# A hybrid decoder block on one core: another order in the opening, whole residual rows and spaced row work at the block ends

## The chip, the core and the metric

The kernel runs on one core of one Trainium2 chip. The metric is device time in microseconds (us) of one execution. The core has a matrix engine (PE, with its weight loads PEld), a vector engine (DVE), a scalar engine (ACT), a general engine (POOL), and a sync engine (SP) whose queue issues nearly all DMAs here. Each engine takes its instructions in the order of its own queue and a waiting instruction holds those behind it.

## The reference, cut to what matters

Two thousand and forty-eight tokens of width 1024 pass one decoder block: a gated mixer of two branches, then a feed-forward part, each with a norm before and after and with scales, shifts and gates made from one conditioning vector `c`.

```python
mod = c @ w_ada + b_ada
shift_m, scale_m, gate_m, shift_f, scale_f, gate_f = split(mod, 6)
h = modulate(rms_norm(x, g_pre_mix), shift_m, scale_m)
q_a, k_a, v_a, q_m, k_m, v_m, o_m, i_m, f_m, g_a, g_m = split(h @ w_in)
q_a, k_a = rope(q_a, positions), rope(k_a, positions)
y_a = sliding_window_attention(q_a, k_a, v_a, attn_sinks)
q_m, k_m = split(silu(causal_depthwise_conv(concat(q_m, k_m), conv_w, conv_b)))
y_m = sigmoid(o_m) * head_layer_norm(mlstm_chunkwise(q_m, k_m, v_m, i_m, f_m), mlstm_norm_w)
mix = (sigmoid(g_a) * (y_a @ w_branch_attn) + sigmoid(g_m) * (y_m @ w_branch_mlstm)) @ w_out
x = x + gate_m * rms_norm(mix, g_post_mix)
h2 = modulate(rms_norm(x, g_pre_ffn), shift_f, scale_f)
x = x + gate_f * rms_norm((silu(h2 @ w_ffn_gate) * (h2 @ w_ffn_up)) @ w_ffn_down, g_post_ffn)
```

## The kernel before, in words

**Tiling.** The mixer runs over four blocks of 512 tokens (`block(b)`); each is four tiles of 128 tokens. The feed-forward part follows over two blocks of 1024 tokens. Every large product is made in three matmuls: weights and activations are split into a rounded part (`whi`, `hhi`) and the rest (`wlo`, `hlo`), and `mm3` adds hi·hi, hi·lo and lo·hi. ACT casts the rounded part (L233, L236), DVE subtracts for the rest (L234, L237), and PE needs both. PSUM holds four `acc` banks and four `mix` banks. SBUF pools used here: nine `big` buffers of 1 MB, six `tx` buffers of 256 KB, nine `tm`, two `raw` weight buffers, four split buffers.

**Order.** A list scheduler sets the order of each engine's queue from the program's order; instructions wrapped in `pin` keep their place. All matmuls and the first rows of block 0 are pinned; later work is interleaved by `spawn`/`tick`: a generator is resumed when the planner's clock `now` (which `mm` and `transpose` advance) has passed the time that it last yielded.

**The opening.** `FirstRows` prepares block 0. Its inputs are `x_first` (two loads of 1 MB), the first eight halves of the conditioning matrix `ada_first` (tile i = 0..3, two halves of 1 MB each: rows k = 0..3 and 4..7 of eight), and `w_q_vm` in pieces of 1 MB. For each tile i the scale and shift of two feature columns (2i, 2i+1) are needed. Part of the eight rows is multiplied on PE as one-column matmuls (`on_pe`, L460: "columns", 128x1 in the profile), part on DVE as an accumulation over 512 elements (`on_v`, L474: L479 for the first term, L482 for the others). `biased` (L468) adds the bias to the PE part, `sums` (L484) adds the DVE accumulation over partitions by four one-column matmuls against `ones` and finishes s1 and sh1 on DVE (L490 to L492), `turned` (L494) transposes the normalised x of the two feature columns on PE, `rows` (L500) applies scale and shift on ACT (L503 gives `hhi`, L506 the unrounded value), `rest` (L508) makes `hlo` on DVE (L510), `cast` and `weights` (L512, L516) split the weights (L514 on ACT, L519 on DVE). `warm(n)` issues n matmuls of `ones` against `ones`. `begin` runs all this for tile 0; `first_group` (L312) then runs the weight matmuls of four pieces (two feature columns each) in thirds hi·hi, lo·hi, hi·lo of eight, and calls `beside(si, third, j)` after every four, which prepares tile si + 1 between them. Each float32 matmul (columns, `ones`, transposes aside) stands in the trace as two records.

**The block end.** `stage5` ends the mLSTM branch, `stage6` starts the next block's normalised input (`hprep`, L593, and `rope_tables`, L684), and `residual_out` (L625) multiplies by `w_o` in two halves of 512 columns. `evac` (L629) squares each result on ACT (L635) and multiplies by the gate on DVE (L639). After the second half of a row `norm_and_add` (L649) makes the norm's factor (POOL's power, L587), loads the row of x in two parts into `tx` buffers (`load_rows`, L674, the DMA is L677), adds gate·norm (DVE L661 for the right half; ACT L663 and POOL L664 for the left), stores (L665) and squares the new row on ACT (L667) for the second norm. In blocks 0 to 2 the whole of it is issued at once; in block 3 it is kept for later (`late`). The next block's first product, on `w_q_vm` (casts L233 in two parts for the pairs of heads), follows on PE at once.

**The streams.** `ada_stream` (L560) loads the rest of the conditioning matrix in parts of 256 KB (L567) and accumulates them on DVE (`ada_terms`, L421, L423) in the same step.

## Time and profile before

| | us |
|---|---|
| median of 3 runs (range) | 2719.85 (2719.6 to 2720.81) |
| the profiled execution, its own time | 2722.81 |
| span of that execution, first to last instruction | 2721.0 |
| start of block 0's key/value product in it, behind the opening | 58.80 |
| mean granted PE clock over the span | 0.996 |

The profiled execution took 1.8 us more than its span, and 2.96 us more than the median of the runs. A row of the timeline gives the start, the duration, the engine, the line, the operation, the tiles written and read, shapes, the count of instructions merged in the row and, in brackets, the idle time of the engine before it with what ended it. A row of the windows gives busy time by engine with the count of instructions, then the granted PE clock, the busy share of the DMA engines and GB/s.

### The profile page before, as it was taken

The page shows a single profiled execution, that of the slowest core. Times are in us where ns is not written, and L with a number is a line of the kernel's source. Part 1 is how long each engine was busy: PE and PEld are TensorE (multiplying, and loading weights), DVE is VectorE, ACT ScalarE, POOL GpSimd, SP SyncE. Part 2 cuts the span into 40 slices and gives each one's busy share as a digit, 9 for nine tenths or more (in the row PEclk, how much of TensorE's full clock was granted, in tenths as well). Part 3 has the DMA queues.
Part 4 walks back from the last instruction along what each step waited for, and adds up shares of the span by engine and source line. Part 5 has one row for each costly group of instructions (what it writes and reads, how often), then busy time and mean ns, then how long its engine had stood idle before and what let it go on. Part 6 is the DMA issues. An engine that isn't in the chain of part 4 may idle for free.

```text
span 2721.0 us, 35220 instructions
## 1 busy us (share of the span) xinstructions
PE 2691.2 (99%) x12788; PEld 2217.6 (81%) x12788; DVE 1915.7 (70%) x3765; ACT 1233.1 (45%) x2277; POOL 217.6 (8%) x241
## 2 busy tenths in 40 slices
PE   9999999999999999999999999999999999999998
PEld 8778887788787888878887888888887888888887
DVE  6778567687686876668747777777678666676566
ACT  4543454533555346564334333335555333333553
POOL 0101211011210012110111000000010000000000
PEclk8999999999999999999999999999999999999999
DMA  5332352242543434434357454446577323334655
GB/s 218 111 132 95 113 193 98 86 135 94 174 143 108 159 119 167 159 106 151 139 201 266 137 173 149 165 161 225 194 240 239 116 86 112 100 109 153 224 188 193
DMA packets 189646, 417.32 MB, mean 153 GB/s; under 512 B 14088, under 2 KB 85392, under 8 KB 172832
## 3 DMA queue, kind: packets, MB, share of 16 engines
q1 hardware_dynamic: 189328, 415.00, 44.5%
q8 instruction: 100, 1.64, 0.2%
q14 instruction: 74, 0.61, 0.1%
q10 hardware_dynamic: 144, 0.08, 0.0%
HBM read 331.11 MB, written 83.92 MB: 153 GB/s over the span
## 4 chain that ended last, share of the span: by engine, by line
PE 83%; issue 5%; DVE 5%; DMA 4%; ACT 2%; POOL 1%; SPq 0%; DVEq 0%; POOLq 0%; ACTq 0%
PE acc L174 57%; PE mix L174 24%; PE mix L179 2%; DMA tx<-in_x_dram 1%; DMA ob<-x 1%; DVE hl L1270 1%; DMA tx<-in_ada_rest_dram 1%; DMA big<-in_x_dram 0%; DMA x<-tx 0%; DMA hc_d<-os 0%; DVE wlo L237 0%; DMA raw<-as_d 0%; ACT whi L236 0%; POOL rs L587 0%; DVE w L1655 0%
## 5 line engine op out<-in xcount | busy, mean ns | idle before, releaser
L236 ACT CAST whi<-raw 128x1024 fp32r<-128x1024 f32 (+1 forms) x208 | 211.7, 1019 | 434.5 <-PE acc L174 363.8
L174 PE MATMUL acc<-hhi,wlo 128*128 128x512 f32 x896 | 354.3, 395 | 1.0 <-DVE wlo L237 1.0
L174 PE MATMUL acc<-hhi,whi 128*128 128x512 f32 x896 | 352.8, 394 | 0.8 <-ACT whi L236 0.8
L174 PE MATMUL acc<-hlo,whi 128*128 128x512 f32 x896 | 351.6, 392 | 0.0
L237 DVE TENSOR_TENSOR wlo<-raw,whi 128x1024 fp32r<-128x1024 f32 (+1 forms) x208 | 251.1, 1207 | 139.4 <-ACT whi L236 138.2
L174 PE MATMUL acc<-big,hl 128*128 128x512 f32 x1056 | 253.7, 389 | 0.0
L1269 ACT CAST hl<-raw 128x512 fp32r<-128x512 f32 x274 | 165.2, 621 | 185.1 <-PE mix L174 110.3
L174 PEld LDWEIGHTS acc<-big,hl 128*128 128x128 f32 x1056 | 198.1, 188 | 41.1
L1270 DVE TENSOR_TENSOR hl<-raw,hl 128x512 fp32r<-128x512 f32 x274 | 184.3, 688 | 41.9 <-ACT hl L1269 39.7
L174 PEld LDWEIGHTS acc<-hhi,wlo 128*128 128x128 f32 x896 | 168.3, 188 | 37.8 <-DVE wlo L237 1.5
L174 PEld LDWEIGHTS acc<-hhi,whi 128*128 128x128 f32 x896 | 168.4, 188 | 36.2 <-ACT whi L236 1.6
L174 PEld LDWEIGHTS acc<-hlo,whi 128*128 128x128 f32 x896 | 168.3, 188 | 34.8
L174 PE MATMUL mix<-big,hl 128*128 128x512 f32 x704 | 195.8, 389 | 0.0
L174 PE MATMUL acc<-whi,big 128*128 128x512 f32 x512 | 164.6, 394 | 1.1 <-ACT whi L236 1.0
L174 PE MATMUL acc<-big,whi 128*128 128x512 f32 x512 | 157.6, 392 | 0.0
L174 PEld LDWEIGHTS mix<-big,hl 128*128 128x128 f32 x704 | 132.1, 188 | 27.4
L587 POOL TENSOR_TENSOR rs<-ms,nhalf 128x1 f32<-128x1 f32 (+1 forms) x40 | 31.6, 792 | 1399.6 <-DVE ms L584 1392.3
L174 PE MATMUL acc<-hl,hl 128*128 128x512 f32 x564 | 135.7, 391 | 0.0
L174 PE MATMUL acc<-wlo,hhi 128*128 128x512 f32 (+1 forms) x384 | 132.1, 360 | 3.1 <-DVE wlo L237 2.3
L174 PE MATMUL mix<-hc,hl 128*128 128x512 f32 x528 | 134.0, 389 | 0.0
L174 PE MATMUL acc<-whi,hlo 128*128 128x512 f32 (+1 forms) x384 | 132.1, 359 | 0.0
L174 PE MATMUL acc<-whi,hhi 128*128 128x512 f32 (+1 forms) x384 | 126.0, 370 | 4.8 <-ACT whi L233 3.2
(339 smaller groups left out, 5512.9 us busy)
## 6 DMA issues: line engine op xcount, KB each, us to landing
raw<-in_w_cols_dram SPq DMA_DIRECT2D x56, 1024.0 KB
as_d<-w SPq DMA_DIRECT2D x154, 256.0 KB
raw<-in_w_ffn_up_dram SPq DMA_DIRECT2D x22, 1024.0 KB
raw<-as_d SPq DMA_DIRECT2D x42, 512.0 KB
raw<-in_w_q_vm_dram SPq DMA_DIRECT2D x16, 1024.0 KB
tx<-in_ada_rest_dram SPq DMA_DIRECT2D x64, 256.0 KB
raw<-in_w_o_dram SPq DMA_DIRECT2D x16, 1024.0 KB
hc_d<-os SPq DMA_DIRECT2D x28, 512.0 KB
```

The lines of the kernel that those rows point to most:

```text
L174: return pin(T.matmul(o, lhsT=lhsT, rhs=rhs, start=start, stop=stop, skip_group_check=resumed))
L179: pin(T.transpose(o, i, ident[:k, :k]))
L236: A.copy(hv, src)
L237: eng.tensor_tensor(lv, src, hv.bitcast(F32), op=ALU.subtract)
L587: G.tensor_tensor(r[:, :n], ms[:, :n], nhalf[:, :n], op=ALU.pow)
L1269: A.copy(v(hi), src)
L1270: V.tensor_tensor(v(lo), src, v(hi).bitcast(F32), op=ALU.subtract)
```

## The change

**Opening.** `load_ada` loads one half at a time; the first weight piece is loaded in two parts (0.5 MB each) with the first half of tile 1 between them. For tile 0, PE takes rows 0 and 1 alone (instead of 0 to 3), and each column is followed by a `ones` matmul in another bank; DVE takes rows 2 to 7, the bias is added ahead of the last row, the transposes stand ahead of the sums, five `ones` matmuls behind them. Tile 1's columns move from `begin` to behind the first eight weight matmuls. In `beside`, bias, sums and rows move one step ahead (to (1, 1)), the columns of the next tile behind the last matmuls of the piece.

**Block ends, blocks 0 to 2.** Residual rows are loaded as two `big` tiles of 256 whole rows during the first half of `w_o`; row work (`whole_rows`) is spawned per row with pauses of 1.5 us and 3 us of the planner's clock and stores a whole row in one DMA. `hprep` is cut by pauses, its last one (L_X) 3 us instead of 16. The next block's rope tables are spawned during the gate projection (`table_steps`), and their two sine activations (`sines`) stand in `stage5`.

**Streams.** `ada_stream` yields 3 us of the planner's clock between a load and its use; the gain row is loaded with the bias row.

```diff
-L_X, L_HT = 16000.0, 1400.0
+L_X, L_HT = 3000.0, 1400.0
...
                 if ordered:
                     rows0.later.append((lk, sv, hk))
-                    if len(rows0.later) < 3:
-                        rows0.cast(rows0.later[-1:])
+                    if rows0.begun:
+                        rows0.cast(rows0.later[-1:], pin)
...
+            src = w[c0 // 512, k0 // 4]
+            if ordered and not k0 and not c0:
+                pin(nc.sync.dma_start(t[:, :2], src[:, :2]))
+                load_ada(1, 0)
+                pin(nc.sync.dma_start(t[:, 2:], src[:, 2:]))
+            else:
+                pin(nc.sync.dma_start(t, src))
...
-        def on_pe(self, i, ks):
+        def on_pe(self, i, ks, between=False):
             pt = self.pt[i] = mix_tile()
+            pw = mix_tile() if between else None
...
+                        if between:
+                            mm(pw[:, :P], ones, ones, True, True)
...
         def begin(self):
+            self.begun = True
             self.scaled()
-            self.on_pe(0, range(4))
-            self.warm(4)
-            self.on_v(0, range(4, 8))
+            self.on_pe(0, (0, 1), True)
+            self.on_v(0, (2, 3, 4, 5, 6))
             self.biased(0)
+            self.on_v(0, (7,))
+            self.turned(0)
             self.sums(0)
-            self.turned(0)
+            self.warm(5)
+            self.cast(self.later[:2], pin)
             self.rows(0)
             self.cast(self.later[2:], pin)
-            self.on_pe(1, (0, 1))
+            self.on_v(1, (2, 3))
             self.weights()
-            self.on_v(1, (2, 3, 4))
+            self.on_v(1, (4, 5))
             self.rest(0)
-            self.on_v(1, (5,))
             self.on_v(1, (6, 7))
...
+            elif (third, j) == (0, 1):
+                if i == 1:
+                    self.on_pe(1, (0, 1))
             elif (third, j) == (1, 1):
                 self.turned(i)
-            elif (third, j) == (2, 0):
                 self.biased(i)
                 self.sums(i)
                 self.rows(i)
                 self.weights()
+                if i < 3:
+                    self.on_v(i + 1, (2, 3, 4))
             elif (third, j) == (2, 1):
+                self.rest(i)
                 if i < 3:
                     self.on_pe(i + 1, (0, 1))
-                    self.on_v(i + 1, (2, 3, 4))
-                self.rest(i)
-                if i < 3:
                     self.on_v(i + 1, (5, 6, 7))
...
+                    yield 3000.0
                     ada_terms(acc, raw, k0, 2)
-                    yield gap
+                    yield gap - 3000.0
...
-            rest = norm_and_add(t, y)
             if late is None:
-                for _ in rest:
-                    pass
+                spawn(whole_rows(t, y), 0.0)
             else:
-                late.append(rest)
+                late.append(norm_and_add(t, y))
+
+        def whole_rows(t, y):
+            ss = st["ss"]
+            s = small.tile([P, 1], F32, tag="ss1", name=nm("ss1"), bufs=4)
+            V.tensor_tensor(s, ss[:, t:t + 1], ss[:, 4 + t:5 + t], op=ALU.add)
+            r = rsqrt_of_sumsq(s, 1)
+            sx = small.tile([P, 2], F32, tag="sx", name=nm("sx"), bufs=4)
+            row, y0 = st[t // 2][:, t % 2, :], st["keep"][:, t, :]
+            yield 1500.0
+            V.scalar_tensor_tensor(row[:, 512:], y, r[:, 0:1], row[:, 512:], op0=ALU.mult, op1=ALU.add)
+            A.activation(y0, y0, AF.Copy, scale=r[:, 0:1])
+            G.tensor_tensor(row[:, :512], y0, row[:, :512], op=ALU.add)
+            nc.sync.dma_start(dst[t * P:(t + 1) * P, :], row)
+            yield 3000.0
+            for h2 in range(2):
+                A.activation(y0, row[:, h2 * 512:(h2 + 1) * 512], AF.Square, accum_out=sx[:, h2:h2 + 1])
...
+            for n, piece in enumerate(token_group(srcs_rows(w, nk, hf * 512), nk, 512, lhs, lambda t, ps, hf=hf: evac(hf, t, ps))):
+                if late is None and not hf and n >= 2:
+                    yield lambda i=n - 2: st.update({i: resid(i)})
+                yield piece
...
+            if b + 1 < NBLK and i == 3:
+                yield lambda: R.update(tb=spawn(table_steps(b + 1)))
...
+            if b + 1 < NBLK:
+                finish([R["tb"]])
+                sines(b + 1)
...
-    run(program(), {0: chunks(0), 1: chunks(1), 2: chunks(2, 3)})
+    run(program(), {0: halves((0, 0), (0, 1)), 1: halves((1, 1), (2, 0), (2, 1)), 2: halves((3, 0), (3, 1))})
```

How the queues change is shown at three places; the numbers behind a tile's name count buffers, and differ between the two programs.

PE before, in the opening (`big_274` is the first half of tile 0, `big_280` that of tile 1, `tm_328` the DVE accumulation, `big_90` and `big_92` are x):

```order
L174 MATMUL mix_186<-ones 128x128 x32
L174 MATMUL mix_306<-vec,big_274 128x1 x16
L174 MATMUL mix_323<-ones 128x128 x4
L174 MATMUL mix_336<-ones,tm_328 128x1 x4
L179 MATMUL mix_344<-ident,big_90 128x128 x2
L179 MATMUL mix_344<-ident,big_92 128x128 x2
L174 MATMUL mix_362<-vec,big_280 128x1 x8
L174 MATMUL acc_382<-whi_286,hhi_184 128x512
```

PE of the change at the same place, from the last column of tile 0 (`tm_323` is the accumulation; the transposes are those of L176):

```order
L171 MATMUL mix_305<-vec,big_274 128x1
L171 MATMUL mix_306<-ones 128x128
L176 MATMUL mix_333<-ident,big_90 128x128 x2
L176 MATMUL mix_333<-ident,big_92 128x128 x2
L176 MATMUL mix_338<-ident,big_90 128x128 x2
L176 MATMUL mix_338<-ident,big_92 128x128 x2
L171 MATMUL mix_343<-ones,tm_323 128x1 x4
L171 MATMUL mix_351<-ones 128x128 x5
L171 MATMUL acc_378<-whi_291,hhi_184 128x512
```

The transposes have moved ahead of the sums, and no column of tile 1 stands ahead of the first weight matmul any more; its eight columns stand behind the eighth.

SP before at the end of block 0 (L265 loads weights, L677 the parts of residual rows, L665 stores, L861 is the next block's key/value weight):

```order
L265 DMA raw_3472<-in_w_q_vm_dram 128x2048
L677 DMA tx_3526<-in_x_dram 128x512
L677 DMA tx_3532<-in_x_dram 128x512
L677 DMA tx_3558<-in_x_dram 128x512
L677 DMA tx_3564<-in_x_dram 128x512
L665 DMA x_0_163<-tx_3532 128x512
L665 DMA x_0_163<-tx_3526 128x512
L861 DMA raw_3643<-in_w_kv_dram 128x2112
L677 DMA tx_3590<-in_x_dram 128x512
```

SP of the change there (L116 loads whole rows, the first row here still for the next block's input, then the two of the residual; L268 loads weights, L575 is the conditioning stream, L675 stores a row):

```order
L116 DMA big_3170<-in_x_dram 128x2x1024
L116 DMA big_3246<-in_x_dram 128x2x1024
L116 DMA big_3293<-in_x_dram 128x2x1024
L268 DMA raw_3154<-in_w_o_dram 128x2048
L268 DMA raw_3244<-in_w_o_dram 128x2048
L575 DMA tx_3329<-in_ada_rest_dram 128x512
L575 DMA tx_3413<-in_ada_rest_dram 128x512
L268 DMA raw_3341<-in_w_q_vm_dram 128x2048
L268 DMA raw_3454<-in_w_q_vm_dram 128x2048
L675 DMA x_0_163<-big_3246 128x1024
```

Eight loads that waited their turn for a `tx` buffer behind the weights have become two loads ahead of the last two pieces of `w_o`.

ACT before at that place, from the fourth square of a result (L635) on; L663 is the scaled copy, L667 the square of a new row, L233 the cast of the next block's weights:

```order
L635 ACTIVATE tx_3611,ss_3303<-acc_3366 128x512
L667 ACTIVATE big_3304,sx_3557<-tx_3558 128x512
L663 ACTIVATE big_3304<-big_3304,rs_3587 128x512
L667 ACTIVATE tx_3581,sx_3589<-tx_3596 128x512
L233 CAST whi_3678<-raw_3472 128x2x4x64 x2
L667 ACTIVATE big_3304,sx_3589<-tx_3590 128x512
L233 CAST whi_3708<-raw_3472 128x2x4x64 x2
```

ACT of the change, from the fourth square (L652) to the same cast (L230); L673 is the scaled copy, L678 the square of a row:

```order
L652 ACTIVATE tx_3583,ss_3301<-acc_3346 128x512
L673 ACTIVATE big_3302<-big_3302,rs_3552 128x512
L678 ACTIVATE big_3302,sx_3537<-big_3246 128x512
L673 ACTIVATE big_3302<-big_3302,rs_3573 128x512
L678 ACTIVATE big_3302,sx_3537<-big_3246 128x512
L678 ACTIVATE big_3302,sx_3554<-big_3246 128x512 x2
L678 ACTIVATE big_3302,sx_3575<-big_3293 128x512
L673 ACTIVATE big_3302<-big_3302,rs_3591 128x512
L678 ACTIVATE big_3302,sx_3575<-big_3293 128x512
L678 ACTIVATE big_3302,sx_3593<-big_3293 128x512
L230 CAST whi_3665<-raw_3454 128x2x4x64 x2
```

Three instructions stood between the fourth square and the third cast of weights; now ten do, and none of them reads a `tx` buffer. From 1885 us of the span before at the latest (DVE from 1308, ACT from 1380, PE from 1745), the queues hold the same instructions in the same order in both programs.

More of the change, by code (lines that the diff above doesn't have):

```diff
@@ L117, in load_x, with load_ada @@
         return xb
-    def load_ada(c0):
-        halves = []
-        for half in range(2):
-            t = big([8, 256])
-            pin(nc.sync.dma_start(t, a["ada_first"][c0 // 256, half]))
-            halves.append(t.rearrange("p (k u) c -> p k u c", u=2))
-        return halves
+    def load_ada(i, half):
+        t = big([8, 256])
+        pin(nc.sync.dma_start(t, a["ada_first"][i, half]))
+        ada_raws[i].append(t.rearrange("p (k u) c -> p k u c", u=2))
     x_first = [load_x(x_d, big, i) for i in range(2)]
@@ L134, in decoder_block @@
     c_sb, b_if, sinks = col("c", 0, KD), col("b_if", 0, 8), col("sinks", 0, HQ)
-    ada_raws = []
+    ada_raws = [[] for _ in range(4)]
     ident = const.tile([P, P], F32, name="ident")
@@ L235, in split @@
         else:
-            A.copy(hv, src)
-            eng.tensor_tensor(lv, src, hv.bitcast(F32), op=ALU.subtract)
+            pin(A.copy(hv, src))
+            pin(eng.tensor_tensor(lv, src, hv.bitcast(F32), op=ALU.subtract))
         return hv, lv
@@ L389, in decoder_block, with ada_tail @@
     gg_f_d = tc.dram_tile([P, D], F32, name="gg_f_d")
-    def ada_tail(acc, part, ch, kind):
+    def ada_tail(acc, part, ch, kind, gb=None):
         c0 = part * D + ch * 256
@@ L431, in __init__ @@
             self.later = []
+            self.begun = False
         def norms(self):
@@ L681, in decoder_block @@
     x1 = [tc.dram_tile([TB, D], F32, name=f"x1_{b}") for b in range(NBLK)]
-    def rope_tables(b):
-        for _ in table_steps(b):
-            pass
     def table_steps(b):
@@ L742, in table_steps, with sines @@
         V.scalar_tensor_tensor(cos, sin, -1.0, sin, op0=ALU.mult, op1=ALU.min)
-        yield
+        tables[b] = sin, cos
+        if not b:
+            yield
+            sines(b)
+    def sines(b):
+        sin, cos = tables[b]
         A.activation(sin, sin, AF.Sin)
         A.activation(cos, cos, AF.Sin, bias=half_pi[:, 0:1])
-        tables[b] = sin, cos
     kth = kvp.tile([P, P + TB], F32R, name="kth")
@@ L1185, in evac_gm @@
             A.copy(big_of(("gm", i // 4))[:, i % 4, :], ps)
-        yield from feature_tiles(a["w_cols"], KD, 2560, KD, rhs_h, evac_gm)
+        for i, piece in enumerate(feature_tiles(a["w_cols"], KD, 2560, KD, rhs_h, evac_gm)):
+            if b + 1 < NBLK and i == 3:
+                yield lambda: R.update(tb=spawn(table_steps(b + 1)))
+            yield piece
         def stage5():
@@ L1772, in decoder_block, with halves @@
     F["ahead"] = next(second)
-    def chunks(*which):
-        return lambda: ada_raws.extend(load_ada(256 * i) for i in which)
-    run(program(), {0: chunks(0), 1: chunks(1), 2: chunks(2, 3)})
+    def halves(*which):
+        return lambda: [load_ada(i, half) for i, half in which]
+    run(program(), {0: halves((0, 0), (0, 1)), 1: halves((1, 1), (2, 0), (2, 1)), 2: halves((3, 0), (3, 1))})
     open_ffn()
```

34 lines of the change are left out of this document (22 added, 12 removed).

## The prediction

> **What bounds the kernel now.** First the page: PE is the engine that is nearly always busy. Then the waits of PE, to see how much time others cost it at all.
>
> ```profile
> PE 2691.2 (99%) x12788; PEld 2217.6 (81%) x12788; DVE 1915.7 (70%) x3765; ACT 1233.1 (45%) x2277; POOL 217.6 (8%) x241
> PE acc L174 <- DVE wlo L237: 4.6, 4, 1.6
> ...
> PE acc L174 <- ACT hhi L503: 0.3, 1, 0.3
> ```
>
> The thirteen rows of the waits sum to 21.4 us, none of them over 4.6. So a change of order can win only two things: these waits, and time in which PE is "busy" with something other than the model's products or at a lower clock. The second lies in the opening; third view, the timeline of PE from the start, with the windows for the clock.
>
> ```profile
> 15.46 2.06 PE L174 MATMUL mix<-ones 128*128 128x128 f32 x8
> 17.31 1.71 PE L174 MATMUL mix<-ones,tm 128*128 128x1 f32 x8
> 20.61 3.41 PE L174 MATMUL mix<-vec,big 128*128 128x1 f32 x16
> 23.89 3.76 PE L174 MATMUL acc<-whi,hhi 128*128 128x512 f32 x8
> 34.96 3.38 PE L174 MATMUL acc<-whi,hhi 128*128 128x512 f32 x8
> 43.63 1.84 PE L174 MATMUL mix<-vec,big 128*128 128x1 f32 x16
> 45.33 2.09 PE L174 MATMUL acc<-whi,hhi 128*128 128x512 f32 x8
> 53.24 2.09 PE L174 MATMUL acc<-whi,hhi 128*128 128x512 f32 x8 [0.34 <-ACT hhi L503]
> 58.80 0.28 PE L174 MATMUL acc<-whi,hhi 128*128 128x264 f32 x1
> 11.00:15.50 4.50, 4.50 (x37) 4.50 (x35) 2.48 (x7) 4.25 (x5) 0.71 (x1) 0.82 1.04 431
> 15.50:23.90 8.40, 8.40 (x42) 8.40 (x42) 5.10 (x14) 4.95 (x8) 0.00 (x0) 0.50 1.01 418
> 35.00:38.20 3.20, 3.20 (x10) 2.52 (x11) 3.17 (x5) 0.43 (x1) 0.00 (x0) 0.57 0.80 314
> 38.20:58.80 20.60, 20.26 (x114) 17.16 (x113) 14.61 (x40) 8.93 (x15) 0.00 (x0) 1.00 0.16 52
> ```
>
> The first weight matmul starts at 23.89, behind columns that it doesn't need (3.41 us); and PE, though busy in every microsecond, has half its clock from 15.5 to 23.9, still in the group that follows, and again from 35 to 38, each time behind one-column matmuls. Eight weight matmuls take 3.4 to 3.8 us there and 2.1 us at full clock, so the two slow groups cost 1.7 + 1.3 = 3.0 us. The four pieces start at 23.89, 34.96, 45.33 and 53.24.
>
> **The change: the opening.** What feeds tile 0:
>
> ```profile
> 13.50 0.49 DVE L479 TENSOR_SCALAR tm<-big,vec 128x512 f32<-128x512 f32 x1 [1.88 <-DMA big<-in_ada_first_dram]
> 14.02 2.33 DVE L482 SCALAR_TENSOR_TENSOR tm<-big,vec,tm 128x512 f32<-128x512 f32 x3
> 19.05 0.16 DVE L490 TENSOR_TENSOR s<-mix,ms 128x2 f32<-128x2 f32 x1 [2.57 <-PE mix L174]
> 22.49 0.75 DVE L482 SCALAR_TENSOR_TENSOR tm<-big,vec,tm 128x512 f32<-128x512 f32 x1 [0.63 <-DMA big<-in_ada_first_dram]
> 23.16 1.29 DVE L510 TENSOR_TENSOR hlo<-tx,hhi 128x512 fp32r<-128x512 f32 x2
> 11.00 4.25 ACT L452 ACTIVATE big<-big,rs 128x1024 f32<-128x1024 f32 x4
> 17.60 1.14 ACT L514 CAST whi<-raw 128x512 fp32r<-128x512 f32 x2 [2.35 <-DMA raw<-in_w_q_vm_dram]
> 20.01 1.63 ACT L503 ACTIVATE hhi<-mix,sh,s 128x512 fp32r<-128x512 f32 x2 [1.27 <-PE mix L179]
> ```
>
> DVE now makes six terms instead of four. Two of them (0.49 + 0.78 us) fit into its idle 1.88 us ahead of 13.50; four remain behind the landing (4 x 0.78), with two small adds for the bias (0.1 each, after the 0.16 of such an add) between: done at 16.85, where four terms (0.49 + 2.33) ended at 16.3. PE then has the transposes behind it and does the sums and five `ones` (ten records). At half clock that is 1.6 + ten times 0.23 (eight took 1.85 from start to start), and the first weight matmul starts at 20.8; at full clock the sums take half, scale and shift 0.5 on DVE (three of 0.16), the first `hhi` 0.8 on ACT, and it starts at about 19.4. Either way 3.1 to 4.5 us before 23.89. The weight cast is no obstacle: with the load halved its data needs 0.5 MB less than what landed at 17.60.
>
> What is late next is tile 1. Seven megabytes stand ahead of, and with, its second half in both programs, so I leave its landing at 22.49. DVE then has two terms (1.5), `hlo` (1.3) and two terms (1.5): 26.9. PE arrives there after eight matmuls, the moved columns, eight matmuls and the transposes, at 26 to 27. So PE and DVE meet; sums, eight matmuls and the columns of tile 2 (0.8 + 1.9 + 1.7 at full clock, the last from 43.63 to 45.33) follow, and the second piece starts at about 31.6, 3.4 us before 34.96. The later pieces go by what the third and fourth took at full clock: 53.24 - 45.33 less the 0.34 waited = 7.57, plus 1.7 where columns are in it, and 5.56 for the last. 31.6 + 9.3 + 7.6 + 5.6 = 54.1 against 58.80: **4.7 us**, if the clock stays whole. The eight more `ones` between the columns and the fifth behind cost nothing as long as the second half lands at 13.50: sixteen column and sixteen `ones` records end before the transposes can start, which wait for ACT's last scaled row (15.25). Without that cover they would cost 9 matmuls of 0.46 us at half clock, 4.1 us.
>
> A stretch at half clock costs 1.3 to 1.7 us, as the two slow groups did. Columns stand ahead of 23.89, of 34.96 and of 45.33, and only the first two groups were slow; so what stands there now lies near the limit, and the new order spreads the columns and sums rather than thinning the matmuls around them. I count a third of such a stretch: **-4.2 us**, bounds -1.3 (two more stretches) and -5.
>
> **The block ends.** One chain shows the mechanism, at the end of block 0; then PE's own rows for the others.
>
> ```profile
> 391.43 1.26 DVE L661 SCALAR_TENSOR_TENSOR tx<-tx,rs,tx 128x512 f32<-128x512 f32 x1 [2.92 <-DMA tx<-in_x_dram]
> 392.73 0.63 ACT L667 ACTIVATE tx<-tx 128x512 f32<-128x512 f32 x1 [2.39 <-DVE tx L661]
> 394.01 1.19 PE L174 MATMUL acc<-whi,hhi 128*128 128x512 f32 x4 [1.70 <-ACT whi L233]
> 380.45 0.72 ACT L663 ACTIVATE big<-big,rs 128x512 f32<-128x512 f32 x1 [0.50 <-POOL rs L587]
> 379.87 0.55 POOL L587 TENSOR_TENSOR rs<-ms,nhalf 128x1 f32<-128x1 f32 x1 [35.17 <-DVE ms L584]
> 381.25 1.31 POOL L664 TENSOR_TENSOR tx<-big,tx 128x512 f32<-128x512 f32 x1 [0.83 <-ACT big L663]
> 405.98 0.49 DVE L423 SCALAR_TENSOR_TENSOR acc_ada<-tx,vec,acc_ada 128x256 f32<-128x256 f32 x1 [1.78 <-DMA tx<-in_ada_rest_dram]
> 410.75 0.39 PE L174 MATMUL acc<-wlo,hhi 128*128 128x264 f32 x1 [1.57 <-DVE wlo L237]
> 690.94 1.28 ACT L744 ACT_TABLE_LOAD   x1
> 693.83 0.50 PE L174 MATMUL acc<-whi,big 128*128 128x512 f32 x1 [1.04 <-ACT whi L236]
> 703.11 0.50 PE L174 MATMUL acc<-wlo,big 128*128 128x512 f32 x1 [1.26 <-DVE wlo L237]
> 750.36 0.96 PE L174 MATMUL acc<-whi,hhi 128*128 128x512 f32 x3 [1.47 <-ACT whi L233]
> 903.28 0.48 DVE L423 SCALAR_TENSOR_TENSOR acc_ada<-tx,vec,acc_ada 128x256 f32<-128x256 f32 x1 [3.09 <-DMA tx<-in_ada_rest_dram]
> 908.38 0.50 PE L174 MATMUL acc<-hhi,wlo 128*128 128x512 f32 x1 [1.02 <-DVE wlo L237]
> 1105.14 0.50 PE L174 MATMUL acc<-wlo,hhi 128*128 128x512 f32 x1 [0.76 <-DVE wlo L234]
> ```
>
> A late residual row stops DVE, DVE stops ACT's square, and the square stands ahead of the cast that PE needs. With whole rows loaded during the first half of `w_o` that chain is gone, but ten ACT instructions now stand ahead of the cast, the last of them a square that waits for POOL's fourth add. Followed through with these durations: PE wants the cast at 392.3 (394.01 less 1.70), 48 matmuls of 0.23 (5.56 for 24) behind the end of `w_o`, which is then 381.3. A copy, a pair of casts and the square itself (0.72 + 1.14 + 0.8, a square being 0.63 and the reading of its sum) put the fourth square's end at 384.0. Three copies and five squares later, at 390.2, the last row's left half is scaled; POOL's add of 1.31 ends at 391.5, the last square at 392.3, the cast's first half at 392.9. So 1.70 becomes about 0.7, and likewise 1.47 and 0.76: together -2.0. The two waits at 693 and 703 come from the rope tables, whose sines hold ACT ahead of a cast, and from a stream's load; the tables leave that place: 2.30 becomes 0.5, -1.8. The waits at 410 and 905 to 908 (1.57, 1.02 and a smaller one) come from a stream's load that DVE waited for, 1.78 and 3.09 us; 3 us between load and use covers the one and nearly all of the other: -2.2. One more table load on ACT and larger row loads I price at nothing, as ACT is idle 55% of the time; should one land ahead of a cast it costs the 1.3 us of such a load once. Sum **-6.0 us**, bounds 0 (all waits come back elsewhere) and -8.8 (all rows above gone).
>
> The total, -4.2 - 6.0 = -10.2, is made against the profiled execution (2722.8 with the 1.8 us around its span); taken off the median of the runs, 2719.85, which is 3.0 lower, it gives **2709.6**.
>
> **The rivals.** *The clock falls anyway* (0.17): the mix is too thin, two more windows at half clock, opening only -1.3, total -7.3: 2712.6. For it: columns between `ones` still leave half of the slots with one column, and two slow groups after busy stretches are on record. [...]
>
> *The waits only move* (0.17): the cast still stands behind row work and the streams still wait, block ends 0, opening -4.2: 2715.6. For it: the queue rows show ten instructions where three stood. This is also the case in which half of the change doesn't do what it says.
>
> *Everything goes* (0.10): -5 and -8.8, and some small waits with them: 2705.
>
> *Slower* (0.06): the four rows serialise at each of three block ends. Per row a power, a copy, an add and two squares one after the other are 0.55 + 0.7 + 1.3 + 1.6 = 4.2 us; four in a row from 380.5 end at 397.3, and the cast is 5.6 us late instead of 1.7, 3.9 more at each of three ends, 11.7. With the opening at -4.2 and the streams unhelped that is +7.5: 2727.4. It turns the sign from 1.4 us more at each end on. Against it: the pauses interleave the rows, and the queue shows squares of one row between copies of others.
>
> **How the numbers follow.** Forecast 0.50 at 2709.6. A measurement of this kernel can tell about 0.2%, 5.4 us, from no change: 2714.4 to 2725.3 counts as the same. Faster takes the forecast, the first and the third rival, less a little at the edge: 0.75; the same 0.19; slower 0.06. The range, 2704 to 2716.5, holds all but the slow case and the edges.
>
> **What would show it.** In the changed profile the first weight matmul should start at 19.4 to 20.8 and the key/value product at 54 to 56; the granted clock should be 1.00 in a window over the group that now runs at 34.96. The third cast at the end of block 0 should no longer follow a wait for a load from x, and PE's waits there should be under 1 us. DVE's waits of 1.8 and 3.1 us for the streams should be gone. It is wrong if the second piece waits for tile 1 beyond 33, if the cast is later against PE than before, or if a new wait of over 1 us stands in the middle of a block.

## The result, and the profile after

| | before | after |
|---|---|---|
| median of the runs, us | 2721.58 (2719.60 to 2726.77, six runs) | 2707.86 (2707.38 to 2712.34, six runs) |
| ratio of after to before | | 0.9946, 95% interval 0.9936 to 0.9957 |
| profiled execution, us | 2722.81, span 2721.0 | 2707.94, span 2706.2 |
| mean granted clock of TensorE | 0.996 | 0.998 |

The changed kernel is faster by 0.54%. With three more runs, taken beside those of the change, the median of before is 1.7 us above the one that the prediction started from. Between the medians lie 13.7 us, between the spans of the two profiled executions 14.8.

The waits of PE in the changed kernel, largest first (engine and line that waited, what it waited for: us in total, times, longest one):

```profile
PE mix L171 <- DVE hl L1318: 2.8, 4, 1.6
PE acc L171 <- DVE wlo L231: 2.1, 1, 2.1
PE mix L176 <- DVE ob L1416: 1.9, 1, 1.9
PE acc L171 <- ACT tm L838: 1.6, 2, 1.4
PE acc L171 <- DVE wlo L234: 1.4, 1, 1.4
...
PE acc L171 <- ACT whi L230: 0.5, 1, 0.5
```

Before, the low halves `wlo` cost 5.4 us in five waits (4.6 in four at L237, 0.8 in one at L234). They are now 2.1 and 1.4 us, one wait each, and the 2.1 stands at a place where there was none. The casts `whi` cost 3.2 and 1.8 us in this view before and are down to 0.5. All rows of the view sum to 16.4 us, before to 21.4.

PE's timeline at the opening (start, busy us, engine, line, operation, out<-in, sizes, count, and in brackets the idle time ahead of the row and what ended it):

```profile
14.78 1.30 PE L176 MATMUL mix<-ident,big 128*128 128x128 f32 x8
16.88 1.06 PE L171 MATMUL mix<-ones,tm 128*128 128x1 f32 x8 [0.79 <-DVE tm L486]
17.80 2.48 PE L171 MATMUL mix<-ones 128*128 128x128 f32 x10
19.94 2.63 PE L171 MATMUL acc<-whi,hhi 128*128 128x512 f32 x8
22.41 1.84 PE L171 MATMUL mix<-vec,big 128*128 128x1 f32 x16
...
31.43 2.11 PE L171 MATMUL acc<-whi,hhi 128*128 128x512 f32 x8
...
53.35 0.28 PE L171 MATMUL acc<-whi,hhi 128*128 128x264 f32 x1
...
61.20 0.39 PE L171 MATMUL acc<-wlo,hhi 128*128 128x264 f32 x1 [1.38 <-DVE wlo L234]
```

The first weight matmul stands at 19.94 (before 23.89), the second piece at 31.43 (34.96), the key/value product at 53.35 (58.80). The last row, in the key/value product, waits 1.38 us; before, the same wait was 0.76.

The end of block 0, VectorE's rows first and PE's row behind them, then the windows (busy us of PE, PEld, DVE, ACT and POOL with counts, granted clock of PE, share of the DMA engines, GB/s):

```profile
388.33 0.15 DVE L598 TENSOR_SCALAR ms<-sx 128x1 f32<-128x1 f32 x1
390.75 0.49 DVE L423 SCALAR_TENSOR_TENSOR acc_ada<-tx,vec,acc_ada 128x256 f32<-128x256 f32 x1 [2.26 <-DMA tx<-in_ada_rest_dram]
391.15 0.68 DVE L231 TENSOR_TENSOR wlo<-raw,whi 128x512 fp32r<-128x512 f32 x1
```
```profile
388.61 1.19 PE L171 MATMUL acc<-whi,hhi 128*128 128x512 f32 x4
391.89 0.50 PE L171 MATMUL acc<-wlo,hhi 128*128 128x512 f32 x1 [2.08 <-DVE wlo L231]
```
```profile
389.80:393.20 3.40, 1.32 (x7) 1.07 (x7) 2.46 (x6) 0.93 (x2) 0.00 (x0) 1.00 1.03 404
393.20:396.60 3.40, 3.40 (x10) 2.62 (x9) 1.76 (x5) 0.00 (x0) 0.93 (x1) 0.50 0.97 333
396.60:400.00 3.40, 3.40 (x16) 2.80 (x15) 0.71 (x1) 0.63 (x1) 0.00 (x0) 1.00 0.99 384
```

The four matmuls at 388.61 use the third cast, and they carry no bracket: the wait of 1.70 us is gone. But a new one of 2.08 us follows: on VectorE a term of the modulation stream (L423) stands ahead of the low half that PE needs, and it waits 2.26 us for its load while the DMA engines are full (share 1.03). In the 3.40 us behind, PE has half its clock: 10 matmul records where the next window has 16.

Where the time went, by the start of the same matmul in both traces (counting the 512-column ones from the start, at places where, apart from the opening, the same matmuls lie behind in both):

| matmul | before | after | difference |
|---|---|---|---|
| first | 23.9 | 19.9 | -4.0 |
| 450th | 171.2 | 167.5 | -3.6 |
| 1500th (block 1, behind the end of block 0) | 459.5 | 455.4 | -4.2 |
| 2800th (behind the end of block 1) | 818.5 | 809.4 | -9.0 |
| 3150th (behind the old waits at 905 to 908) | 910.1 | 899.0 | -11.1 |
| 4350th (behind the end of block 2) | 1244.2 | 1230.9 | -13.3 |
| last | 2712.5 | 2698.2 | -14.3 |

So the opening keeps 3.6 us, the end of block 0 gives hardly anything, and blocks 1 and 2 give 9. The last 1.0 us is one wait near 2061 us (1.13 before, 0.15 after), where the order of the instructions is the same in both kernels; in the other kernels below with the changed block ends it is anything up to 1.0 us, so I don't count it for the change.

### The profile page after: what moved, and what is told of

Same layout as the page of the kernel before. It is cut to its first block, busy times and chain, and to the rows that moved or that the text cites. A ratio compares the mean times of both kernels' runs of the same rounds, so it can differ in the third digit from the quotient of the medians.

```text
span 2706.2 us, 35176 instructions
## 1 busy us (share of the span) xinstructions
PE 2681.6 (99%) x12790; PEld 2212.3 (82%) x12790; DVE 1922.9 (71%) x3767; ACT 1235.7 (46%) x2278; POOL 219.7 (8%) x241
## 4 chain that ended last, share of the span: by engine, by line
PE 92%; DVE 4%; DMA 2%; issue 1%; ACT 1%; POOL 0%; SPq 0%; DVEq 0%; POOLq 0%; ACTq 0%
PE acc L171 66%; PE mix L171 24%; PE mix L176 2%; DMA ob<-x 1%; DVE hl L1318 1%; DMA big<-in_ada_first_dram 0%; DMA tx<-in_ada_rest_dram 0%; DVE w L1703 0%; POOL rs L601 0%; DVE big L1318 0%; DMA raw<-in_w_ffn_gate_dram 0%; DVE wlo L234 0%; DVE big L672 0%; DVE w L1689 0%; POOL tm L1024 0%
## 5 line engine op out<-in xcount | busy, mean ns | idle before, releaser
L233 ACT CAST whi<-raw 128x1024 fp32r<-128x1024 f32 (+1 forms) x208 | 211.9, 1019 | 423.1 <-PE acc L171 357.1
L234 DVE TENSOR_TENSOR wlo<-raw,whi 128x1024 fp32r<-128x1024 f32 (+1 forms) x208 | 253.1, 1217 | 164.2 <-ACT whi L233 162.5
```

What stands on the lines that cost most here:

```text
L233: pin(A.copy(hv, src))
L234: pin(eng.tensor_tensor(lv, src, hv.bitcast(F32), op=ALU.subtract))
```

## The experiments

All comparisons are with the kernel before, run beside each on the same chip. Five of the twelve kernels tell the parts apart, three look for what frees the casts, four try to win back the new waits. Runs of one kernel spread over 2 to 13 us, so beside each median stand the waits in its trace.

**Opening alone, and everything but the opening** (the diffs are the parts of the change; shown is one place of each):

```diff
-            self.on_pe(0, range(4))
-            self.warm(4)
-            self.on_v(0, range(4, 8))
+            self.on_pe(0, (0, 1), True)
+            self.on_v(0, (2, 3, 4, 5, 6))
...
```

> The kernel before with the edits of the opening alone (halved first load, columns mixed with ones, terms and sums moved); block ends, streams and tables as before. Theory: the key/value product stands at about 53.4 us as with the whole change (5.4 us earlier than before), the two larger waits behind it (at about 59.5 and 68.3 us) are there too, since they come of PE being early, and the time is 3 to 4.5 us under before. Rival A: those two waits come from the tables' new steps, so that without them nothing is given back and the time is 5 to 6 us under before. Rival B: the opening is worth nothing at the end because a later wait takes it up: within 1.5 us of before.

```diff
+                    yield 3000.0
                     ada_terms(acc, raw, k0, 2)
-                    yield gap
+                    yield gap - 3000.0
...
-            rest = norm_and_add(t, y)
+                spawn(whole_rows(t, y), 0.0)
...
```

> The kernel before with everything but the opening: residual rows loaded whole, row work spaced, tables in steps, streams loaded ahead. Theory: the parts add up, so 9 to 11 us under before; the key/value product stays at 58.8 us; the wait of about 2.1 us for a stream's term at the end of block 0 is there. Rival: the two parts need each other (the new alignment of loads comes from the shorter opening): 5 to 8 us under before, with waits at the block ends left that the whole change doesn't have.

Opening alone: 2718.68 us against 2724.39, ratio 0.9982 (0.9973 to 0.9991). Everything else alone: 2712.32 us, ratio 0.9956 (0.9943 to 0.9968), in its trace 13.2 us up to the last matmul. The parts add up, within what the runs can tell: 0.18% and 0.44% against 0.54%. (Of the 13.2 us, 1.3 are there already at the key/value product, at 57.5 instead of 58.8, with one stretch at half clock less in the opening; the mean granted clock is 0.997 against 0.996.)

The two waits behind the opening are there with the opening alone (1.39 and 1.45 us at 66.1 and 74.9 us) and not without it (0.75 and 0.96), so they do not come from the tables' new steps, although the time of the opening alone, 4.9 us under before by the ratio and 5.7 by the medians, lies nearer to rival A. That they come of PE being early, as the theory has it, is not shown: in this trace the product starts at 58.2, only 0.55 us earlier than before, and the waits are as long as in the changed kernel. What differs is VectorE's queue. Its rotary rows, which stand ahead of the low half, begin 3.9 us behind the product's start in both kernels with the new opening (62.19 and 58.24 here, 57.29 and 53.35 in the changed kernel), and 3.0 us behind it before (61.76 and 58.80).

The theory missed one thing more: it put the product at 53.4. The windows say why it stands at 58.2:

```profile
21.40:25.40 4.00, 4.00 (x28) 3.60 (x29) 2.69 (x5) 0.74 (x2) 0.00 (x0) 1.00 1.00 420
25.40:28.80 3.40, 2.18 (x16) 1.83 (x15) 2.26 (x9) 0.21 (x1) 0.00 (x0) 1.00 1.01 417
28.80:39.10 10.30, 10.30 (x34) 8.73 (x33) 6.30 (x12) 3.60 (x6) 0.00 (x0) 0.50 0.68 282
39.10:45.00 5.90, 5.90 (x42) 5.29 (x41) 2.94 (x8) 2.52 (x4) 0.00 (x0) 1.00 0.00 0
```

With a whole clock PE reaches the sums of tile 1 at 25.8, waits 1.2 us for VectorE, and 3.4 us in which PE is busy for 2.18 are followed by 10.2 us at half clock: 5.1 us lost. Of the eleven runs of this kernel eight took 2717.3 to 2720.0 us and three 2723.7 to 2724.1. Only the first of these three was traced, and its last matmul starts 1.7 us later than that of before. So the gain of the opening has a draw in it; that the other two long runs drew the same is likely, and not shown.

**No ones between the columns:**

```diff
-            self.on_pe(0, (0, 1), True)
+            self.on_pe(0, (0, 1))
```

> The changed kernel without the sixteen matmuls of ones between the first columns of tile 0; all else as changed. Theory: columns alone let the clock fall, so a second stretch of about 3.4 us at half clock stands ahead of or over the first weight matmuls, and the time is 1 to 3 us over the changed kernel (10.5 to 12.5 us under before). Rival: the clock depends on other matmuls there, and the order alone (fewer columns ahead of the first weight matmul) does it: within 0.5 us of the changed kernel, granted clock as in it.

2708.74 us, ratio 0.9943 (0.9932 to 0.9955): by the ratio no slower than the changed kernel, so the time is the rival's, while the clock did what the theory says. The half clock came earlier and lasted longer (6.83 us from 14.55, where the changed kernel has 3.41 from 17.73), and the first weight matmul starts at 20.64 instead of 19.94. But the key/value product starts at 53.78, 0.4 us later than in the changed kernel, and by 132 us nothing is left of it. What PE loses ahead of 25 us it would have waited for tile 1.

**The streams without their lead, and with a longer one:**

```diff
-                    yield 3000.0
                     ada_terms(acc, raw, k0, 2)
-                    yield gap - 3000.0
+                    yield gap
...
```

> The changed kernel with the streams' loads used in the step that issues them, as before. Theory: DVE's waits for a stream come back at about 405 and 900 us, PE waits 2 to 3 us more in all: 11 to 12 us under before. Rival: with whole residual rows the loads are in time anyway, and the wait at the end of block 0, where a stream's term stands ahead of a weight's low half, is the lead's own: it goes, and the time is 1 to 3 us under the changed kernel (14.5 to 16.5 under before).

```diff
-                    yield 3000.0
+                    yield min(gap - 2000.0, 7000.0)
                     ada_terms(acc, raw, k0, 2)
-                    yield gap - 3000.0
+                    yield gap - min(gap - 2000.0, 7000.0)
```

> The changed kernel with 7 us instead of 3 us in the schedule between a stream's load and its use where the stream's step is 9 or 12 us, 3 us where it is 5. On VectorE the third load's terms then stand behind the first two low halves of the third weight piece of block 1. Theory: PE's wait for a low half at about 389 us (2.1 us in the changed kernel) falls under 0.5 us, no stretch at half clock follows it, and the time is 2 to 3.7 us under the changed kernel. Rival: the low half waits for something else (the cast, or the next term), and 1 us or more is left there; time within 1 us.

Without the lead (the gain row, too, is loaded where it is used, as before): 2711.19 us, ratio 0.9958 (0.9945 to 0.9970). The stream's wait near 892 is back on VectorE (2.14 us), and of PE's 1.02 there 0.51. The wait that was expected near 405 does not come back. At the end of block 0 the stream's term stands ahead of the low half without the lead too; VectorE's row and PE's:

```profile
389.93 0.48 DVE L426 SCALAR_TENSOR_TENSOR acc_ada<-tx,vec,acc_ada 128x256 f32<-128x256 f32 x1 [1.28 <-DMA tx<-in_ada_rest_dram]
```
```profile
391.07 0.51 PE L171 MATMUL acc<-wlo,hhi 128*128 128x512 f32 x1 [1.09 <-DVE wlo L231]
```

So the lead did not put it there. The size of this wait differs from execution to execution: in the kernel with no ones between the columns, whose VectorE queue holds the same rows at this place, VectorE waits 0.26 us for the load and PE not at all. The other waits that the trace without the lead has more (1.06 at 447 and 0.90 at 1038) stand in traces with a lead too (1.37 at 449 with the longer one, 1.22 and 1.32 near 1036 and 1040), so I don't put them down to it; and between the opening and PE's last matmul one stretch at half clock stands in each trace, near 1847 here and at 393 in the changed kernel. What is shown of the lead is thus 0.51 us near 897. The median is 3.3 us above that of the changed kernel, but the intervals overlap: that the lead earns the 2 to 3 us expected is not shown.

With 7 us: 2711.31 us, ratio 0.9954 (0.9939 to 0.9969), and PE's wait for the low half is 1.63 us behind another of 0.91, so more lead doesn't mend the end of block 0. VectorE's rows with the longer lead:

```profile
387.91 0.15 DVE L598 TENSOR_SCALAR ms<-sx 128x1 f32<-128x1 f32 x1
390.53 1.00 DVE L423 SCALAR_TENSOR_TENSOR acc_ada<-tx,vec,acc_ada 128x256 f32<-128x256 f32 x2 [2.47 <-DMA tx<-in_ada_rest_dram]
...
391.75 1.29 DVE L231 TENSOR_TENSOR wlo<-raw,whi 128x512 fp32r<-128x512 f32 x2
```

A pause in the code is schedule time, not chip time: now two terms of one load stand there and wait 2.47 us, in place of one that waited 2.26. The expected theory falls for this edit: I had moved the third load's terms, and the second's took their place.

**The tables where they were:**

```diff
-                yield lambda: R.update(tb=spawn(table_steps(b + 1)))
+                pass
...
-                finish([R["tb"]])
-                sines(b + 1)
...
+                for _ in table_steps(b + 1):
+                    pass
+                sines(b + 1)
```

> The changed kernel with the rope tables and their sines computed in one go where they stood before, ahead of the residual work. Theory: in block 1 the sines and their table load stand ahead of a cast again, and PE waits about 1.0 and 1.3 us near 685 and 694 us as it did before; the time is about 2 us over the changed kernel. Rival: those waits went with the streams' loads, and the table's place is worth nothing: no wait of over 0.5 us there, time within 1 us.

2712.11 us, ratio 0.9961 (0.9947 to 0.9975). ScalarE's queue in it, and PE:

```profile
684.44 1.28 ACT L786 ACT_TABLE_LOAD   x1
685.73 0.31 ACT L786 ACTIVATE sin<-sin 128x128 f32<-128x128 f32 x1
685.95 0.39 ACT L787 ACTIVATE cos<-cos,half_pi 128x128 f32<-128x128 f32 x1
686.24 1.03 ACT L233 CAST whi<-raw 128x1024 fp32r<-128x1024 f32 x1
```
```profile
687.32 1.20 PE L171 MATMUL acc<-whi,big 128*128 128x512 f32 x4 [1.04 <-ACT whi L233]
```

The table load and the sines stand ahead of the cast again and PE waits the same 1.04 us as before. The second wait (1.26 before) isn't back; nor is it in the kernel without the lead, where the tables stand as changed. With the opening alone, where neither edit is in, it is 0.27 us, so what removes it is not isolated. The theory is half right: the tables' place is worth about 1 us.

**What frees the cast.** Three kernels: the load issued late in the code, no pauses, and, from the other side, whole rows alone put into the kernel before.

```diff
-                if late is None and not hf and n >= 2:
-                    yield lambda i=n - 2: st.update({i: resid(i)})
...
+            if t % 2 == 0:
+                st[t // 2] = resid(t // 2)
             row, y0 = st[t // 2][:, t % 2, :], st["keep"][:, t, :]
```

> The changed kernel with the two residual loads of blocks 0 and 1 issued where the row work begins, and not during the first half of w_o; all row work as changed. Theory (the early load is what frees the cast at the block end): the casts behind the end of blocks 0 and 1 are late again, PE waits 1.5 to 5 us more at about 388 and 741 us, and the time is 3 to 8 us over the changed kernel. Rival (the spacing of the row work does it): PE's waits at the block ends stay as they are in the changed kernel, within 1 us of it.

2708.34 us, ratio 0.9947 (0.9932 to 0.9962), PE's waits for the casts 0.12 and 0.52 us as in the changed kernel: the rival's side, no loss. (The edit acts on block 2 as well as on blocks 0 and 1.) The trace shows that the edit moved the load little, from about 331 to 343.8 us, still some 30 us ahead of the row work. In the kernel before the half rows go into small buffers that the streams and the row work use too, and their loads are issued as late as this:

```profile
373.45 6.86 SPq L677 DMA_DIRECT2D tx<-in_x_dram  x4
384.22 0.81 SPq L677 DMA_DIRECT2D tx<-in_x_dram  x2
392.04 0.33 SPq L677 DMA_DIRECT2D tx<-in_x_dram  x1
393.13 0.38 SPq L677 DMA_DIRECT2D tx<-in_x_dram  x1
```

What these loads waited for before, from 366 to 412 us (us in total, times, longest): squares that write into a small buffer, and a store out of one.

```profile
SPq L677 <- ACT tx L635: 5.3, 2, 4.5
SPq L677 <- DMA x<-tx: 4.3, 1, 4.3
```

```diff
-                spawn(whole_rows(t, y), 0.0)
+                for _ in whole_rows(t, y):
+                    pass
...
-L_X, L_HT = 3000.0, 1400.0
+L_X, L_HT = 16000.0, 1400.0
...
-                yield 1500.0
```

> The changed kernel without the pauses in the row work and in the preparation of the next block's rows; residual rows still loaded whole into the big buffers. The late loads have shown that the place of the load in the code is worth nothing, which leaves two theories for the casts that are in time at the block ends. Spacing: without the pauses squares and scaled rows stand ahead of the casts again, PE waits 1.5 us or more at about 388 and at 741, time 2 to 5 us over the changed kernel. Buffers: it is that the rows have buffers of their own and need not wait for a free small one; the waits at 388 and 741 stay under 0.7 us and the time is within 1.5 us.

2708.12 us, ratio 0.9945 (0.9932 to 0.9957): no wait at 388 or 741 at all. The spacing isn't it either. What it trades is small: 0.38 and 0.30 us come at 404 and 408, and 1.16 at 796; the wait of 2.08 at 392 is not there, and a stretch at half clock stands near 1452.

```diff
-            rest = norm_and_add(t, y)
             if late is None:
-                for _ in rest:
-                    pass
+                whole_row(t, y)
...
+            row, y0 = st[t // 2][:, t % 2, :], st["keep"][:, t, :]
+            V.scalar_tensor_tensor(row[:, 512:], y, r[:, 0:1], row[:, 512:], op0=ALU.mult, op1=ALU.add)
+            A.activation(y0, y0, AF.Copy, scale=r[:, 0:1])
+            G.tensor_tensor(row[:, :512], y0, row[:, :512], op=ALU.add)
...
```

> The kernel before with one part of the change: in blocks 0 and 1 the residual rows are whole, loaded two at a time into the large buffers, and the row work goes through them in place; no pauses, no early load in the code, opening, streams and tables as before. Theory (by elimination, since neither the load's place nor the pauses count): this alone takes PE's waits for a cast at about 392 us (1.70) and 748 us (1.47) under 0.7 us each, and the time falls by 2.5 to 6 us under before. Rival: early load and pauses can stand in for each other, and without both the cast is late: 1.4 us or more stay at both places, time within 1.5 us of before. The waits at about 693 and 703 stay (tables), as do those at 905 to 908 (streams).

2718.82 us against 2722.83, ratio 0.9985 (0.9976 to 0.9994); 3.9 us between the spans. SyncE's loads and PE at both places, and the waits that stay:

```profile
347.78 0.43 SPq L116 DMA_DIRECT2D big<-in_x_dram  x1
...
348.76 0.65 SPq L116 DMA_DIRECT2D big<-in_x_dram  x1
```
```profile
392.25 1.07 PE L174 MATMUL acc<-whi,hhi 128*128 128x512 f32 x4
...
691.44 1.20 PE L174 MATMUL acc<-whi,big 128*128 128x512 f32 x4 [1.04 <-ACT whi L236]
...
700.73 0.50 PE L174 MATMUL acc<-wlo,big 128*128 128x512 f32 x1 [1.28 <-DVE wlo L237]
...
746.68 1.28 PE L174 MATMUL acc<-whi,hhi 128*128 128x512 f32 x4
```

Both waits for a cast (1.70 and 1.47) are gone with this alone; the early place in the code and the pauses are not needed for it. The tables' waits stay, as expected, and of the 1.46 us at 905 to 908 there stay 1.02. But the wait at 410 (1.57 before), which the prediction gave to the streams, is down to 0.28 and 0.31 us at 407 and 412: with the row loads out of the small buffers, the stream's first term comes at 387.1 instead of 398.6. So the whole rows carry the block ends, and the wait at 410 with them. One thing is not separated: the edit puts the rows into buffers of their own and also makes two loads out of eight, and no run has one without the other.

**The stream behind the end of block 0:**

```diff
-                R_ada.append(spawn(ada_stream([(4, "scale"), (3, "shift")], 9000.0)))
...
+            if b == 0:
+                yield lambda: R_ada.append(spawn(ada_stream([(4, "scale"), (3, "shift")], 7000.0), 12000.0))
...
-                    if part == 2 and not ch + k0:
+                    if part in (2, 4) and not ch + k0:
```

> The changed kernel with block 1's modulation stream (the scale and shift of the second norm) started behind the block end: its first load is kept in program order there, and its step is 7 us instead of 9. On VectorE no term of the stream stands ahead of the low halves of the third weight piece of block 1 any more. Theory: PE's wait for a low half at about 389 us (1.1 to 2.1 us in six of seven kernels with the changed block end) falls under 0.5 us, no half-clock stretch follows it, and the time is 2 to 4 us under the changed kernel. Rival: the low half is late because of its cast or of the four rows, and a wait of over 1 us stays there; or the stream's later loads bring back waits further on, near 410 to 450 us or at 905: within 1 us of the changed kernel.

2706.56 us, ratio 0.9940 (0.9927 to 0.9952). PE at the same place:

```profile
389.31 1.20 PE L171 MATMUL acc<-whi,hhi 128*128 128x512 f32 x4 [0.83 <-ACT whi L230]
390.35 0.39 PE L171 MATMUL acc<-wlo,hhi 128*128 128x512 f32 x1
...
405.38 0.39 PE L171 MATMUL acc<-wlo,hhi 128*128 128x264 f32 x1 [1.06 <-DVE wlo L234]
```

The wait of 2.08 us and the half clock behind it are gone, as they should be if the stream's term was their cause (in the kernel with no ones between the columns, where the term's load came in time, they are not there either). But the cast ahead is now late by 0.83 (0.12 with the change) and a wait of 1.06 comes at 405: 1.9 us are won from trace to trace, not 4. It has the lowest median of all, 1.3 us under that of the changed kernel in its own runs; the intervals overlap, and it is not shown to be faster.

**Ones where PE waits in the opening**, at three places, and then at the last of them alone on top of the later stream:

```diff
-    rows0.warm(32)
+    rows0.warm(36)
...
+            self.warm(3)
             self.sums(0)
...
+                if i == 1:
+                    self.warm(4)
                 self.sums(i)
```

> The changed kernel with eleven more matmuls of ones where PE waits in the opening: four more ahead of the first column, three ahead of the sums of tile 0, four ahead of those of tile 1. Theory: the half-clock stretches there come of a window of 3.41 us in which PE streams too little, so with the waits filled no such stretch is left in the opening, the key/value product starts at 52.8 to 53.6 us, and the time is 0 to 2 us under the changed kernel. Rival A: the ones only delay the sums; the product is 0.7 to 1.6 us later. Rival B: the stretch comes anyway (0.50 for 3.41 us or more between 11 and 45 us), so what PE does there isn't what sets it.

> The kernel with the stream behind the block end, and with four matmuls of ones ahead of the sums of tile 1, where PE waits 1.1 to 1.3 us at about 25.8 us whenever the clock is whole before. Theory: that wait falls in a window of 3.41 us with under 1.3 us of wide matmuls in some executions, and then the clock is halved from about 29 us on (opening alone: 10.24 us at half clock from 28.82, product at 58.2 instead of 53.6); filled, the window has enough, the product starts at 53.3 to 54.0 us with no half clock behind 25 us, and the time is 0 to 1.5 us under the kernel with the later stream alone. Rival: the ones delay the sums by 0.9 us and the rest with it: 0.5 to 1 us over it.

All three places: 2708.00 us, ratio 0.9946 (0.9931 to 0.9961), the product at 54.99 with half clock from 14.20 to 17.61: rival A's delay, and rival B's stretch; whether its reading holds too, that what PE does there isn't what sets the clock, is not shown. The last place alone: 2709.30 us, ratio 0.9947 (0.9933 to 0.9961), 2.7 us over the later stream alone, the rival's side, though the intervals overlap. In that trace the clock is whole from the start to PE's last matmul, and the product stands at 53.84:

```profile
25.71 1.06 PE L171 MATMUL mix<-ones 128*128 128x128 f32 x8
27.40 1.02 PE L171 MATMUL mix<-ones,tm 128*128 128x1 f32 x8 [0.62 <-DVE ms L476]
```

No half clock behind 25 us, as expected, but three traces without these ones have none in the opening either (the two with another lead and that with the late loads), so this one trace doesn't show that the ones did it. The window of 3.41 us and the 1.3 us of wide matmuls in the two theories were my estimates from the earlier traces; neither run shows that they set the clock. No time is won: with the clock at half for 3.4 us the changed kernel has the product at 53.35.

## Why the prediction was right, and where its sizes were off

The forecast was 2709.6 us; the median is 2707.86, 1.7 lower and inside the range. The likeliest case came: both parts gain. That the two numbers lie so near is in part luck. The forecast gain was 10.2 us, the measured one is 13.7 between the medians and 14.8 between the traces; with the three later runs the median of before rose by 1.7 us, and taken off that one the same forecast would have been 2711.4. By its steps:

- **The first weight matmul at 19.4 to 20.8**: 19.94, with PE at half clock from 17.73 on, so the step followed the right row (transposes, sums, `ones`). Six traces that begin with a whole clock have 19.2 to 19.4, the forecast for it, though the terms written down for that case add up to 18.95 only.
- **Tile 1 is late next**: right, and stronger than I put it. With the clock whole PE waits 1.1 to 1.3 us there, with it at half it doesn't, and the second piece starts at 31.43 (forecast 31.6).
- **The key/value product at 54.1, -4.7, less a third of a half-clock stretch, so -4.2**: 53.35, so -5.45. The pieces took 0.2 us less each than summed. The deduction was wrong in kind at this place: the stretches ahead of 25 us cost nothing here. Three traces with none have the product at 53.52 to 53.61, three others with 3.41 us at half have it at 53.32 to 53.71, and no ones between the columns with 6.83 us at 53.78. The one of 10.24 us behind 25 us, in the opening alone, cost 5 us.
- **What the step left out**: what is late behind the product. 1.8 of the 5.45 us are given back by the 450th matmul; the two waits in the product and behind it grew by 0.62 and 0.48 us; the other 0.7 is spread over amounts under 0.3 us each, and its cause is open. Net -3.6 against -4.2.
- **The casts at the block ends, -2.0**: the waits went further than priced, 1.70 to 0.12, 1.47 to 0.52, and that of 0.76 is gone: 3.3 us. The mechanism on record (a late residual row stops VectorE, that stops the square, that the cast) agrees with whole rows alone, where the loads go early and the casts are in time. The words "loaded during the first half of `w_o`" named the wrong cause: it is the whole rows in buffers of their own, wherever their loads are written.
- **The tables, -1.8**: both waits are gone, 2.30 us; 1.04 of them are shown to be the tables', what removes the other is open.
- **The streams, -2.2**: the waits at 410 and 905 to 908 are gone, 3.0 us with the smaller one. But the step credited the lead with them, and only 0.51 near 897 comes back without it; the one at 410 went with the whole rows. What the step left out is the other side of that: the stream runs ahead now, and at the end of block 0, where the DMA engines are full (share 1.03), one of its terms stands ahead of a low half, with the lead or without. In this execution that costs 2.1 us and 1.7 more through the clock, half of its 3.41 us. This is the "new wait of over 1 us" that the prediction named as a sign against it.
- **The sum of -6.0** is the term that was mis-sized: 10.7 us are measured from the 450th matmul on, 1.0 of it chance in the last third. Up to the 4350th PE's bracketed waits of over 0.25 us fell from 10.1 us in ten to 3.5 in three, and the half clock took 1.7 back. That makes 4.9 of 9.7. A wait costs somewhat more from matmul to matmul than its bracket (at the cast of 1.70 the starts, at 391.92 and 394.01, lie 2.09 us apart where 0.23 is usual), which is 1.1 us of the rest. The remaining 3 to 4 us are made of amounts under 0.35 us each, in no row that was priced.

## What to carry to other kernels

Where a load comes too late, ask first whose buffer it waits for; its place in the code may mean little to a scheduler that is free to issue it earlier. When one group of loads leaves a pool of buffers, the next one can run ahead in it (here the stream's first term, from 398.6 to 387.1 us), so look where the work on that one will stand. A pause in the code between load and use is schedule time: at the end of block 0 VectorE waited 1.28 us for the load without a pause, 2.26 with one of 3 us (0.26 in another execution) and 2.47 with one of 7. And a gain on the engine that bounds the kernel is kept only until the next wait: here two of them took back 1.1 of 5.45 us.

## What the runs showed of the hardware

In the trace of before PE has half its clock for 13.65 us from 13.86, for 3.41 us from 34.34, and from 2717.22 us to the end; in that of after for 3.41 us from 17.73, for 3.41 us from 393.19, and from 2700.60 us to the end, the last of them in each behind PE's last matmul. Two traces at the same wait, that of a transpose for VectorE's `ob`, in windows as above:

```profile
1843.80:1847.10 3.30, 1.32 (x8) 0.88 (x7) 1.70 (x3) 1.36 (x3) 0.00 (x0) 1.00 1.00 354
1847.20:1850.50 3.30, 3.30 (x10) 2.54 (x9) 2.59 (x5) 1.45 (x3) 0.00 (x0) 0.50 0.23 86
```
```profile
1844.30:1847.60 3.30, 1.50 (x10) 1.13 (x9) 2.01 (x4) 1.67 (x3) 0.00 (x0) 1.00 0.97 340
1847.70:1851.00 3.30, 3.30 (x18) 2.73 (x18) 3.04 (x6) 1.86 (x5) 0.00 (x0) 1.00 0.21 80
```

In the first pair (streams without lead, a wait of 1.98 us) PE is busy for 1.32 of 3.30 us and has half its clock in the window behind; in the second (rows not spaced, 1.80 us) it is busy for 1.50 of 3.30 us and keeps the whole clock. The changed kernel waits 1.89 us there and keeps it too, with PE busy for 1.51 of the 3.40 us from 1841.80. Near 392 half clock came in or behind each of three waits: of 1.63 us (longer lead), of 1.76 (late loads, where the starts of the matmuls from 392.80 to 395.79 lie 0.43 us apart and 0.23 is usual) and of 2.08 (changed kernel, where the 3.41 us at half clock cost 1.7 us on top of the wait). A busy PE didn't always keep its clock either: in the trace of before it is busy in all of the 3.41 us ahead of 13.86 and of the 3.41 us ahead of 34.34, one-column matmuls last in both, and has half its clock behind each. From these cases I give no rule.
